# A decoder block on one core: feed-forward differences moved from GpSimd to VectorE, and one more pair of chunks in the down projection's rounds of seven products

## The chip, the core and the metric

The kernel runs on one core of one Trainium2 chip. The metric is the device time of one execution in microseconds (us): the median of three runs of the kernel before is 1283.06 us (1282.82 to 1283.29). The engines that matter are TensorE (PE in the profile; its weight loads are a row of their own, PEld), VectorE (DVE), ScalarE (ACT), GpSimd (POOL) and SyncE (SP). Each engine executes its own instructions strictly in the order in which the kernel records them, and waits at an instruction until what it needs is there.

## The reference

One layer with a feed-forward half-step at both ends; the mixing part between them is untouched by the change. For 512 tokens, model width 1024 and feed-forward width 2816:

```
def swiglu(x, w_gate, w_up, w_down):
    return (jax.nn.silu(x @ w_gate) * (x @ w_up)) @ w_down

h = h + 0.5 * swiglu(rms_norm(h, g_ffn1[i]), w_ffn1_gate[i], w_ffn1_up[i], w_ffn1_down[i])
...   # convolution module, dilated attention, gated merge
h = h + 0.5 * swiglu(rms_norm(h, g_ffn2[i]), w_ffn2_gate[i], w_ffn2_up[i], w_ffn2_down[i])
h = h + jax.nn.sigmoid(rms_norm(h, g_ple[i]) @ w_ple_gate[i]) * (p[i] @ w_ple_proj[i])
return rms_norm(h, g_final)
```

Inputs and outputs are float32.

## The kernel before

**Precision.** A float32 product is made of three matmuls on rounded halves: each operand is split into a high part (ACT copies it into a rounded type) and a low part (DVE subtracts the high part from the original). The names ending in h and l are these halves: `wh`, `wl` of a weight slab, `bh`, `bl` (or `b`, both halves in one tile) of a moving operand, `hidh`, `hidl` of a hidden chunk.

**Chunks and pairs.** The feed-forward width is 22 chunks of 128 channels, taken as 11 pairs. Gate and up are computed for a pair at a time. Pairs 0 and 1 are computed plainly (keys "gq"), while the norm is still being made. Pairs 2 to 10 are computed with seven products in place of eight (keys "gu"): the weights and the tokens are cut in two halves each way, sums and differences of the quarters are formed, and the products have the names B11, B21, T2, T1, T3, B22, T4, in this order. `quarters_of` (L712, L713, L715) records the matmuls of one product, each 128x256; a gate/up product works on four slabs of the model width and has 24 of them. Results go to three PSUM banks, pa (B11, then T2 on top, then T3, then T4), pe (B21) and pd (T1, then B22 on top). A product that accumulates on a bank may start only when the sum before has been read from it.

**The down projection** is done in `ROUNDS`, four entries (first pair, number of pairs). Round 0 is plain (`down_plain`, keys "dp"): for each of eight row blocks m, the 128x512 matmuls of all chunks of the round go to one bank (pd), and DVE adds it to the residual (L966). Rounds 1 to 3 use the seven products again (`down`, keys "dn"), in two groups of four row blocks, so 14 products a round; a product on k pairs has 6k matmuls of 128x256. After each product DVE adds the bank to the residual (`add`, L727, or L723 and L730 as two halves).

**The order** is written out by hand in `PLAN`: before, gate/up of pairs 2 to 5, round 1, pairs 6 to 8, round 2, pairs 9 and 10, the plain round, round 3. The feed-forward is executed twice with the same plan.

**Forming a pair.** A pair that goes into rounds of seven needs seven moving operands: `form_pair` makes four differences of 256 columns (`sub`, L643, two into each tile `t`) and four splits (`put`: ACT at L655, DVE at L658): B11, B21 with B22, T1 with T2, T3 with T4. Before, the differences are executed by GpSimd (`by=FORMS`, and FORMS is G). The 13 pieces of a pair are put in a list `later`; `gate_up` records some of them behind each product (`QUOTA`, 17 for a gate/up step), `down_plain` up to three behind each m, and `down` of rounds 1 and 2 takes none on its own: it only records, before a product, whatever that product still lacks. The last pair before a round is held back and formed at the start of the next gate/up step. A pair of the plain round is only split (`keep`, ACT L747 and DVE L749).

**Weights.** Slabs come by DMA from SP. For T2, T1, T3 and B22 DVE forms sums of quarters (L342, L346, L350, L355; names `s`, `wr`) and the low halves `wl` (L405), ACT the high halves (L404). For B11, B21 and T4, and for the plain round, the low half is made by ACT (L374, minus the high half) and a DMA from GpSimd's queue that adds the raw weights onto it (L376). The width of these instructions is 1024 for gate/up and for a round of four pairs, 768 for a round of three.

**Other work in the way.** In the first feed-forward the rotary tables are made by some 40 DVE instructions at L1024 (`tables`, tiles ang, n, e, nh, nl), recorded one behind several of the products and one behind each m of the plain round, from round 2 on.

## Time and profile before

| | us |
|---|---|
| median of three runs | 1283.06 |
| profiled execution, first to last instruction (span) | 1280.8 |
| TensorE busy, share of the span | 1267.4, 99% |
| VectorE busy | 1015.3, 79% |
| ScalarE busy | 740.9, 58% |
| GpSimd busy | 299.8, 23% |
| granted TensorE clock, mean | 0.998 |

The profile gives the profiled execution's own time as its span; the 2.3 us between the span and the median lie outside the first and the last instruction. The stages follow one another on TensorE: in the first feed-forward, gate/up of pair 2 starts at 52.09 us, round 1 begins near 133 us, the plain round runs from 294.52 to 317.05 us and round 3 ends near 347.9 us. In the second feed-forward the plain round runs from 1158.11 to 1180.65 us. The timeline lists each instruction by its start; matmuls are pipelined, so the distance between two starts is the pace, and the listed duration of one is its latency. DVE instructions overlap a little in the same way.

### The profile page before, as it was taken

Reading aid. Unit: us, or ns where it says so; the run is one execution under the profiler, and the core shown is the slowest. Engines: PE = TensorE matmul, PEld = TensorE weight load, DVE = VectorE, ACT = ScalarE, POOL = GpSimd, SP = SyncE. Lnnn points to the kernel's source line nnn. Section 1 sums busy time; section 2 is a strip of 40 time slices with the busy share of each in tenths; the row PEclk is TensorE's granted clock in tenths of the full one; section 3 lists DMA queues with packets and bytes.
Section 4 is the critical chain, followed back from the end, with each engine's and each line's share of the span. In section 5 each row is a group of like instructions: output and inputs, shape, how many; then the busy total and the mean of one; then the engine's idle time right before and its main releaser. Section 6 shows DMA issues by size and latency. Waiting matters only on the chain.

```text
span 1280.8 us, 21791 instructions
## 1 busy us (share of the span) xinstructions
PE 1267.4 (99%) x8266; PEld 1163.6 (91%) x8266; DVE 1015.3 (79%) x1617; ACT 740.9 (58%) x1088; POOL 299.8 (23%) x392
## 2 busy tenths in 40 slices
PE   9999999999999999999999999999999999999997
PEld 7899999998988888989898888898899999998986
DVE  6988778898969887878778755786988888786875
ACT  6677566575643264746565445373677566585662
POOL 3122222132223232333232222012122122132000
PEclk9999999999999999999999999999999999999999
DMA  9676876867879889898887788657576876867641
GB/s 302 148 171 161 204 201 157 206 165 191 193 177 227 213 152 204 155 188 150 173 183 166 168 190 218 160 119 211 132 177 159 203 206 146 208 168 187 155 115 50
DMA packets 114128, 226.12 MB, mean 177 GB/s; under 512 B 20584, under 2 KB 50664, under 8 KB 114024
## 3 DMA queue, kind: packets, MB, share of 16 engines
q0 software_dynamic: 49600, 142.10, 54.6%
q1 hardware_dynamic: 64136, 82.37, 20.1%
q8 instruction: 65, 1.06, 0.3%
q14 instruction: 39, 0.32, 0.1%
q10 hardware_dynamic: 288, 0.26, 0.1%
HBM read 168.56 MB, written 2.13 MB: 133 GB/s over the span
## 4 chain that ended last, share of the span: by engine, by line
PE 76%; DVE 2%; issue 0%; ACT 0%; DVEq 0%
PE pa L712 5%; PE pa L713 5%; PE pa L715 5%; PE pq L458 4%; PE pq L459 4%; PE pq L460 4%; PE pg L458 3%; PE pg L460 3%; PE pg L459 3%; PE pd L713 3%; PE pd L715 3%; PE pd L712 3%; PE pb L459 2%; PE pb L460 2%; PE pb L458 2%; PE pe L713 1%
## 5 line engine op out<-in xcount | busy, mean ns | idle before, releaser
L376 POOL DMA_DIRECT2D wl<-wr x108 | 93.4, 867 | 440.4 <-ACT wl L374 341.1
L712 PE MATMUL pa<-bh,wh 128*128 128x256 f32 x680 | 167.6, 284 | 0.5 <-DVE gx L727 0.4
L713 PE MATMUL pa<-bl,wh 128*128 128x256 f32 x680 | 167.3, 283 | 0.0
L1098 DVE SCALAR_TENSOR_TENSOR acc<-glu,taps,acc 128x511 f32<-128x511 f32 (+14 forms) x240 | 161.6, 732 | 0.0
L405 DVE TENSOR_TENSOR wl<-s,wh 128x1024 fp32r<-128x1024 f32 (+1 forms) x96 | 108.5, 1132 | 38.0 <-ACT wh L404 37.8
L374 ACT ACTIVATE wl<-wh 128x1024 fp32r<-128x1024 f32 x84 | 87.9, 1051 | 81.9 <-DMA wh<-in_w_in 50.8
L712 PEld LDWEIGHTS pa<-bh,wh 128*128 128x128 f32 x680 | 130.6, 192 | 1.0 <-issue 0.5
L713 PEld LDWEIGHTS pa<-bl,wh 128*128 128x128 f32 x680 | 130.8, 192 | 0.0
L374 ACT ACTIVATE wl<-wr 128x1024 fp32r<-128x1024 f32 (+1 forms) x108 | 105.7, 979 | 24.3 <-DVE wl L405 11.4
L404 ACT ACTIVATE wh<-s 128x1024 fp32r<-128x1024 f32 (+1 forms) x96 | 93.0, 969 | 38.8 <-PE pd L459 14.7
L388 ACT ACTIVATE wh<-wr 128x1024 fp32r<-128x1024 f32 (+1 forms) x108 | 105.5, 977 | 11.0 <-PE pd L715 6.1
L712 PE MATMUL pd<-bh,wh 128*128 128x256 f32 x448 | 110.3, 284 | 0.0
L713 PE MATMUL pd<-bl,wh 128*128 128x256 f32 x448 | 110.2, 283 | 0.0
L376 POOL DMA_DIRECT2D wl<-in_w_in x56 | 48.5, 869 | 219.6 <-ACT wl L374 200.5
L715 PE MATMUL pa<-bh,wl 128*128 128x256 f32 x680 | 97.0, 283 | 0.0
L458 PE MATMUL pq<-xsh,wh 128*128 128x512 f32 x224 | 88.8, 396 | 0.0
L715 PEld LDWEIGHTS pa<-bh,wl 128*128 128x128 f32 x680 | 88.4, 192 | 0.0
L459 PE MATMUL pq<-xsl,wh 128*128 128x512 f32 x224 | 87.4, 390 | 0.0
L460 PE MATMUL pq<-xsh,wl 128*128 128x512 f32 x224 | 87.4, 390 | 0.0
L713 PEld LDWEIGHTS pd<-bl,wh 128*128 128x128 f32 x448 | 86.2, 192 | 0.0
L712 PEld LDWEIGHTS pd<-bh,wh 128*128 128x128 f32 x448 | 86.1, 192 | 0.1
L458 PE MATMUL pg<-xsh,wh 128*128 128x512 f32 x192 | 76.1, 396 | 0.2 <-ACT xsh L478 0.2
(330 smaller groups left out, 3616.0 us busy)
## 6 DMA issues: line engine op xcount, KB each, us to landing
wl<-wr POOLq DMA_DIRECT2D x72, 512.0 KB, 5.7
wh<-in_w_in POOLq DMA_DIRECT2D x56, 512.0 KB, 7.0
wl<-in_w_in POOLq DMA_DIRECT2D x56, 512.0 KB, 6.0
wr<-in_w_ffn_up SPq DMA_DIRECT2D x80, 256.0 KB, 4.4
wr<-in_w_ffn_gate SPq DMA_DIRECT2D x78, 256.0 KB, 4.8
wr<-in_w_ffn_down SPq DMA_DIRECT2D x96, 192.0 KB, 3.8
wl<-wr POOLq DMA_DIRECT2D x36, 384.0 KB, 4.4
wr<-in_w_ffn_down SPq DMA_DIRECT2D x16, 256.0 KB, 4.1
```

The costliest lines, as they stand in the source:

```text
L374: A.activation(l.bitcast(F32R), h, AF.Copy, scale=-1.0)
L376: G.dma_start(to, src, accum_op=OP.add)
L388: A.activation(h, r, AF.Copy)
L404: A.activation(h, r, AF.Copy)
L405: V.tensor_sub(l, r, h.bitcast(F32))
L458: PE.matmul(ps, wh, xh, start=start, stop=False, skip_group_check=part)
L459: PE.matmul(ps, wh, xl, start=False, stop=False, skip_group_check=part)
L460: PE.matmul(ps, wl, xh, start=False, stop=stop, skip_group_check=part)
L712: PE.matmul(o, h[:, c], th, start=q in ("B11", "B21", "T1") and i == 0, stop=False, skip_group_check=True)
L713: PE.matmul(o, h[:, c], tl, start=False, stop=False, skip_group_check=True)
L715: PE.matmul(o, l[:, c], th, start=False, stop=i >= len(at) - 2, skip_group_check=True)
L1098: bg.append(lambda acc=acc, g=g, w=w, s=s: V.scalar_tensor_tensor(acc[:, s:], g[:, :S - s], w, acc[:, s:], op0=OP.mult, op1=OP.add))
```

## The change

The four differences of a pair in `form_pair` are executed by DVE instead of GpSimd. The plain round of the down projection has one pair (pair 0) instead of two; pair 1, whose gate and up are still computed plainly, is formed at the start of gate/up step 3 and goes into round 1. The rounds of seven products take pairs 1 to 3, 4 to 6 and 7 to 10, so the last has four pairs. The plan moves with them: each round comes one gate/up step earlier, and three gate/up steps lie before the plain round. The pairs held back are 4 and 7 (before 5 and 8). At the start of gate/up step 3 the waiting jobs of the plain gate/up are recorded at once, so that pair 1 is complete.

```
-ROUNDS = ((0, 2), (2, 3), (5, 3), (8, 3))
+ROUNDS = ((0, 1), (1, 3), (4, 3), (7, 4))

-PLAN = (("gu", 2), ("gu", 3), ("gu", 4), ("gu", 5), ("dn", 1, 0), ("dn", 1, 1), ("gu", 6), ("gu", 7), ("gu", 8),
-        ("dn", 2, 0), ("dn", 2, 1), ("gu", 9), ("gu", 10), ("dp", 0), ("dn", 3, 0), ("dn", 3, 1))
+PLAN = (("gu", 2), ("gu", 3), ("gu", 4), ("dn", 1, 0), ("dn", 1, 1), ("gu", 5), ("gu", 6), ("gu", 7), ("dn", 2, 0),
+        ("dn", 2, 1), ("gu", 8), ("gu", 9), ("gu", 10), ("dp", 0), ("dn", 3, 0), ("dn", 3, 1))
+PLAIN = 1
+HELD = (4, 7)
...
-    FORMS = G if FORMS_ else V
...
-    def form_pair(x1, x2, parts_, tile_=None, first_of=None, by=FORMS):
+    def form_pair(x1, x2, parts_, tile_=None, first_of=None, by=V):
...
-            if j >= EARLY:
+            if j >= PLAIN:
                 waiting.append((j, ts, tile_))
                 return
...
-                    if j not in (ROUNDS[1][0] + ROUNDS[1][1], ROUNDS[2][0] + ROUNDS[2][1]):
+                    if j not in HELD:
                         form()
...
             if key[0] == "gu":
-                if key[1] >= KF // 2 - EARLY:
-                    j = key[1] - KF // 2 + EARLY
+                while jobs and key[1] == EARLY + 1:
+                    next_job()
+                for j in range(PLAIN, EARLY) if key[1] == EARLY + 1 else range(PLAIN) if key[1] == KF // 2 - 1 else ():
                     keep(j, early[j])
                     early[j] = None
                 gate_up(key[1])
```

The order of instructions moves at three places on VectorE that the prediction speaks of. In the rows below, gx and h are the residual, L1024 of the kernel before is L1025 of the changed one.

**VectorE, round 1, first group, around the sum of product T1** (the row that reads pd). Before:

```order
L405 TENSOR_TENSOR wl_1715<-s_265_1598,wh_1714 128x768
L342 TENSOR_TENSOR s_283_1718<-wr_1632,wr_1635 128x768
L727 SCALAR_TENSOR_TENSOR gx<-pd_1627,gx 128x2x256
L346 TENSOR_TENSOR s_286_1744<-s_283_1718,wr_1638 128x768
L727 SCALAR_TENSOR_TENSOR gx<-pa_1625,gx 128x2x256
```

Now:

```order
L405 TENSOR_TENSOR wl_1476<-s_235_1357,wh_1475 128x768
L342 TENSOR_TENSOR s_253_1479<-wr_1393,wr_1396 128x768
L727 SCALAR_TENSOR_TENSOR gx<-pd_1388,gx 128x2x256
L346 TENSOR_TENSOR s_256_1505<-s_253_1479,wr_1399 128x768
L658 TENSOR_TENSOR bl_1508<-t_1355,bh_1507 128x512
L727 SCALAR_TENSOR_TENSOR gx<-pa_1386,gx 128x2x256
```

The new row at L658 is the low half of T3 and T4 of pair 3, the last pair of the round. Product T3, which follows T1 on TensorE, reads it.

**VectorE, the opening of the plain round in the first feed-forward.** Before, from the product of the two gated halves (u from p) on:

```order
L890 TENSOR_TENSOR u_3427<-p_3573,p_3536 128x2x256
L1024 SCALAR_TENSOR_TENSOR ang_2767<-n_2768,ang_2767 128x512
L876 TENSOR_TENSOR u_3427<-pa_3424,p_3459 128x2x256
L749 TENSOR_TENSOR hidl_3421<-tu_610,hidh_3420 128x512
L749 TENSOR_TENSOR hidl_3423<-tu_611,hidh_3422 128x512
L342 TENSOR_TENSOR s_566_3704<-wr_3624,wr_3627 128x768
L966 SCALAR_TENSOR_TENSOR gx<-pd_3698,gx 128x512
```

Now:

```order
L890 TENSOR_TENSOR u_3449<-p_3593,p_3557 128x2x256
L749 TENSOR_TENSOR hidl_3443<-tu_379,hidh_3442 128x512
L749 TENSOR_TENSOR hidl_3445<-tu_380,hidh_3444 128x512
L1025 SCALAR_TENSOR_TENSOR e_2536<-n_2533,e_2536 128x512
L876 TENSOR_TENSOR u_3449<-pa_3446,p_3481 128x2x256
L342 TENSOR_TENSOR s_574_3726<-wr_3642,wr_3645 128x1024
L966 SCALAR_TENSOR_TENSOR gx<-pd_3720,gx 128x512
L643 TENSOR_TENSOR t_3735<-u_3449 128x256
L643 TENSOR_TENSOR t_3735<-u_3449,t_3735 128x256
```

The low halves of the plain pair (L749) stand ahead of the row that waits for T4 (L876) instead of behind it, and the differences of pair 10 (L643) stand in VectorE's row.

**VectorE, from the last sums of the plain round to the first sum of round 3, first feed-forward.** Before:

```order
L966 SCALAR_TENSOR_TENSOR gx<-pd_3829,gx 128x512
L1024 SCALAR_TENSOR_TENSOR ang_2767<-nl_2770,ang_2767 128x512
L966 SCALAR_TENSOR_TENSOR gx<-pd_3846,gx 128x512
L1024 SCALAR_TENSOR_TENSOR ang_2767<-nh_2769,ang_2767 128x512
L405 TENSOR_TENSOR wl_3865<-s_577_3753,wh_3864 128x768
L727 SCALAR_TENSOR_TENSOR gx<-pa_3861,gx 128x2x256
```

Now:

```order
L355 TENSOR_TENSOR s_592_3811<-wr_3651,s_583_3761 128x1024
L966 SCALAR_TENSOR_TENSOR gx<-pd_3810,gx 128x512
L1025 TENSOR_SCALAR n_2533<-n_2533 128x512
L966 SCALAR_TENSOR_TENSOR gx<-pd_3821,gx 128x512
L1025 SCALAR_TENSOR_TENSOR ang_2532<-n_2533,ang_2532 128x512
L405 TENSOR_TENSOR wl_3834<-s_583_3761,wh_3833 128x1024
L727 SCALAR_TENSOR_TENSOR gx<-pa_3830,gx 128x2x256
```

The kinds of rows are the same and the slab is 1024 wide instead of 768. From u (L876) to the sum of B11 (the L727 row, on pa) there are now 31 rows on VectorE: five of 1024 columns, five of 256, two TENSOR_SCALAR at L1025, and 19 others of 512. The low half at L405 is that of product T2.

## The prediction

> **What bounds the kernel now.** I read first the page's line of engines, then the list of what TensorE waited for, then TensorE's own timeline for its pace.

> ```profile
> span 1280.8 us, 21791 instructions
> PE 1267.4 (99%) x8266; PEld 1163.6 (91%) x8266; DVE 1015.3 (79%) x1617; ACT 740.9 (58%) x1088; POOL 299.8 (23%) x392
> ...
> PE pd L459 <- DVE hidl L749: 0.6, 2, 0.4
> PE pa L712 <- DVE gx L727: 0.4, 1, 0.4
> PE pa L712 <- DVE p L884: 0.2, 1, 0.2
> ```

> TensorE is the bound nearly everywhere: in the two feed-forwards together it waited about 1.2 us (the last three rows: total, times, longest). So time can come from fewer or cheaper matmuls, and it can go wherever VectorE, off the path today, becomes late for one of them. The pace of matmuls is the distance of starts, not the listed duration:

> ```profile
> 316.38 0.39 PE L458 MATMUL pd<-hidh,wh 128*128 128x512 f32 x1
> 316.60 0.39 PE L459 MATMUL pd<-hidl,wh 128*128 128x512 f32 x1
> 316.83 0.39 PE L460 MATMUL pd<-hidh,wl 128*128 128x512 f32 x1
> 317.05 0.28 PE L712 MATMUL pa<-b,wh 128*128 128x256 f32 x1
> 317.17 0.28 PE L713 MATMUL pa<-b,wh 128*128 128x256 f32 x1
> ```

> A matmul of 512 columns takes 0.2267 us of TensorE (0.68 for three), one of 256 columns 0.12 us.

> **Term 1, the matmuls.** Per feed-forward the change takes one pair out of the plain round: two chunks, eight row blocks, three matmuls, 48 of 512 columns. It adds a pair to 14 products: six matmuls each, 84 of 256 columns. The plain round takes now (windows view; the first figure behind the window is its length):

> ```profile
> 294.52:317.05 22.53, 22.30 (x98) 17.89 (x97) 18.69 (x26) 10.03 (x14) 6.45 (x8) 1.00 0.81 191
> 1158.11:1180.65 22.54, 22.18 (x98) 17.88 (x97) 12.87 (x18) 9.92 (x14) 6.37 (x8) 1.00 0.84 203
> ```

> Its 96 matmuls need 96 x 0.2267 = 21.76, so 0.77 is lost, at its opening, where the low halves of the plain pairs stand behind the row that waits for T4. In the new order they stand ahead of it; I cost the new plain round at 48 x 0.2267 = 10.88 with nothing lost. Then 22.53 - 10.88 = 11.65 goes and 84 x 0.12 = 10.08 comes: -1.57 per feed-forward, -3.1 for both.

> [...]

> **Term 2, the differences on VectorE.** VectorE gets four differences of 256 columns for each pair of the rounds of seven, 4 x 10 pairs x 2 = 80 (72 were on GpSimd). The prices:

> ```profile
> L643 DVE TENSOR_TENSOR t<-sg,t x8: 417/419/421, 815.8 to 834.9; 128x256 f32<-128x256 f32 x8
> L643 POOL TENSOR_TENSOR t<-u x36: 731/1020/1117, 74.6 to 1168.5; 128x256 f32<-128x256 f32 x36
> ...
> L658 DVE TENSOR_TENSOR bl<-u,bh 128x512 fp32r<-128x512 f32 x18 | 30.0, 1667 | 0.0
> L658 DVE TENSOR_TENSOR bl<-t,bh 128x512 fp32r<-128x512 f32 x40 | 26.9, 685 | 1.1 <-ACT bh L655 1.1
> L658 DVE TENSOR_TENSOR b<-u,b 128x256 fp32r<-128x256 f32 x18 | 19.3, 1074 | 0.0
> L658 DVE TENSOR_TENSOR b<-t,b 128x256 fp32r<-128x256 f32 x8 | 3.4, 419 | 0.2 <-ACT b L655 0.2
> ```

> On VectorE the 80 cost 80 x 0.42 = 34 us. But the same split takes 1667 ns where GpSimd works on the same pair and 685 where it does not (1074 and 419 for the narrow one): 18 x 0.98 + 18 x 0.66 = 29.5 us of VectorE come back. VectorE's load in a gate/up step therefore hardly changes, TensorE's 20.16 us (168 x 0.12) cover it, and I cost the move at nothing there; without cover it would be the 4 x 0.33 a pair that are part of term 4. GpSimd's queue keeps only its DMAs, which are no longer behind a difference; no wait of TensorE names one of them, so that is worth nothing. The slabs of the last round are a third larger, those of the plain round half as large, the bytes in all the same.

> **Term 3, T3 of round 1 waits.** In gate/up step 3 two pairs are formed (2 and 1), 26 pieces with 17 taken; nine are left, step 4 adds the 13 of pair 3 and takes 17, so five are left when round 1 begins, among them the split of T3 and T4 of pair 3. Round 1 records them only when T3 asks. On VectorE that is behind the sum of T1, which waits for T1's last matmul, and behind one sum of weights. The rows there today, TensorE and VectorE:

> ```profile
> 141.45 0.28 PE L712 MATMUL pa<-bh,wh 128*128 128x256 f32 x1
> ...
> 142.53 0.28 PE L713 MATMUL pa<-bl,wh 128*128 128x256 f32 x1
> ...
> 142.06 0.68 DVE L727 SCALAR_TENSOR_TENSOR gx<-pd,gx 128x512 f32<-128x512 f32 x1
> 142.66 0.95 DVE L346 TENSOR_TENSOR s<-s,wr 128x768 f32<-128x768 f32 x1
> 143.82 0.69 DVE L727 SCALAR_TENSOR_TENSOR gx<-pa,gx 128x512 f32<-128x512 f32 x1 [0.21 <-PE pa L715]
> ```

> Round 1 comes a step earlier in the new plan, but the distances within it stay. T3 starts at 141.45; its tenth matmul, the first on the third pair's low half, is at 142.53. The new split comes behind the row at 142.66, so at 142.66 + 0.87 (pace of 768 columns, below) = 143.53, and is done 0.69 later, at 144.22. TensorE stands still for 144.22 - 142.53 = 1.7 us. Queued behind it are the rest of T3, B22 and T4, and nothing gives that time back, since TensorE has no idle time after. The second feed-forward has the same new order:

> ```profile
> 996.73 0.28 PE L712 MATMUL pa<-b,wh 128*128 128x256 f32 x1
> ...
> 1006.70 0.95 DVE L346 TENSOR_TENSOR s<-s,wr 128x768 f32<-128x768 f32 x1
> ```

> Round 1 starts at 996.73, T3 four products of 2.16 later at 1005.37, its tenth matmul at 1006.45; the split would end at 1006.70 + 0.87 + 0.69 = 1008.26: 1.8 us. Together +3.5. Bounds: 1.0 each if the sum of weights happens to run ahead (it can't pass in the order, but the row on pd could start 0.4 us sooner, at its product's end, and TensorE's restart is free), 2.5 each if that sum still waits for its DMA.

> **Term 4, VectorE in the short plain round.** TensorE needs 10.88 us for it instead of 22.53, while VectorE has to do the same eight sums, the sums for round 3 (now wider), the table rows, and now the differences. Paces of VectorE from successive starts, where nothing waits:

> ```profile
> 265.23 1.23 DVE L405 TENSOR_TENSOR wl<-s,wh 128x1024 fp32r<-128x1024 f32 x1
> 266.37 1.22 DVE L342 TENSOR_TENSOR s<-wr,wr 128x1024 f32<-128x1024 f32 x1
> ...
> 301.54 0.42 DVE L658 TENSOR_TENSOR b<-u,b 128x256 fp32r<-128x256 f32 x1
> 301.87 0.42 DVE L1024 TENSOR_SCALAR n<-n 128x512 f32<-128x512 f32 x1
> ...
> 309.11 0.68 DVE L1024 SCALAR_TENSOR_TENSOR e<-n,e 128x512 f32<-128x512 f32 x1
> 309.71 0.94 DVE L350 TENSOR_TENSOR wr<-wr,wr 128x768 f32<-128x768 f32 x1
> 310.58 0.68 DVE L966 SCALAR_TENSOR_TENSOR gx<-pd,gx 128x512 f32<-128x512 f32 x1
> ```

> So 1.14 us for 1024 columns, 0.87 for 768, 0.60 for 512, 0.33 for 256 and for a TENSOR_SCALAR. From u (on pa) to the sum of B11 the new row of VectorE has 31 instructions: 5 x 1.14 + 19 x 0.60 + 7 x 0.33 = 19.4 us. Ahead of them:

> ```profile
> 293.23 0.69 DVE L890 TENSOR_TENSOR u<-p,p 128x512 f32<-128x512 f32 x1 [0.70 <-ACT p L889]
> ```

> Three rows of 512 columns follow it now (two low halves, one table row), so u on pa starts at 293.23 + 4 x 0.60 = 295.63 and the sum of B11 is read at 295.63 + 19.4 = 315.0. Product T2 accumulates on the same bank and needs that row, and the low half one row earlier. TensorE would come to T2 at 294.52 + 10.88 + two products of 2.88 = 311.16. It waits 3.9 us. I take +3.9 for the first feed-forward; bounds 2.5 (if the opening loses nothing to the three rows) and 6 (if rows of this stretch wait for ACT or a DMA). In the second there are no table rows: eight fewer in the stretch (six of 512 columns, two at 0.33: 4.3 us) and one ahead of it, so VectorE begins u 0.5 us behind the opening and B11's sum is read at 0.5 + 15.1 = 15.6; T2 comes at 10.88 + 5.76 = 16.64: no wait, with 1.0 to spare.

> One more thing can be late in that stretch: the low half for B21, which ACT makes behind the split of T3 and T4 of pair 10 in its own order, after which a DMA adds to it (issue to landing: median for this size, then least, median and most over all of L376).

> ```profile
> wl<-wr POOLq DMA_DIRECT2D x72, 512.0 KB, 5.7
> ...
> DMA to landing us min/median/max: 3.9/5.5/11.2
> ```

> The last difference comes at 0.5 + 6.9 (12 rows up to it: 2 x 1.14 + 5 x 0.60 + 5 x 0.33) = 7.4 in the second feed-forward, two ACT instructions (some 0.6 and 1.0) and the 5.7 to landing put the half at about 15, and B21 needs it at 10.88 + 2.88 + 16 x 0.12 = 15.7. I take +0.2 for it, bounds 0 and 2; in the first it is later by some 1.5, but ends ahead of T2's wait.

> **Sum.** -3.1 + 3.5 + 3.9 + 0.2 = +4.5 on the span of 1280.8, so 1285.3; the 2.3 us between span and median stay, **1287.5 us**, 0.35% slower. Less than 0.2% (2.6 us) can't be told from no change here.

> **Rivals.**
> 1. Only term 3 waits: VectorE's row in the plain round is shorter than I count, because nothing disturbs it any more and it enters the round early. For it: 29.5 us come back, and VectorE was idle before some rows of the plain round. Against it: the 31 rows have nothing to wait for in my count already, and they sum to 8.5 us more than the round lasts. It decides if VectorE reaches u 4 us sooner, which T4 forbids. 1283.06 - 3.1 + 3.5 = 1283.5, the same as before.
> 2. Neither waits, the other side: the split of T3 and T4 is done before TensorE comes to it, and the round as well, so only term 1 remains: 1283.06 - 3.1 = 1279.9, faster by 0.25%. The point from which it decides is 142.53 of the old trace: the split must be through VectorE by then, but its row stands behind the sum of T1, which reads what ends at 141.45. Only if TensorE's order asked for pair 3 much later would this hold.
> 3. The waits are worse: in both feed-forwards the low half of B21 lands late, since ACT is held in order by differences that come late, and the DMA takes longer than its median. For it: the longest of these DMAs took 11.2. Against it: a wait of T2 in the first feed-forward already covers some 3 us of such a delay. Two or three us more in each plain round give 1287.3 + 4 to 6, 1291 to 1293.
> 4. The change doesn't do what it says to VectorE: the long splits (1667 ns) have another reason than GpSimd, and 29.5 us don't come back. For it: GpSimd still issues DMAs from the same engine. Against it: the splits of differences (685) ran while it issued some. Then a pair costs VectorE 1.6 us more (0.98 + 0.66); a gate/up step still hides that, the first plain round does not: 1287.5 + 1.6 = 1289.1.

> **How the numbers follow.** The forecast with both waits 0.62, rival 1 0.13, rival 2 0.07, rivals 3 and 4 together 0.18. The range reaches down to rival 1 and up into rival 3: 1283 to 1291.5; outside it are rival 2 and the end of rival 3. Faster 0.07 (rival 2), the same 0.18 (rival 1 and the low end of the forecast, below 1285.6), slower 0.75.

> **What would show it.** Right: round 1 with a gap of 1.5 to 2 us inside T3 in each feed-forward, released by DVE at L658; a gap of about 4 us ahead of T2 of round 3 in the first only, released by L727 or L405; the plain round near 10.9 with no gap at its opening; no split above 0.75 us. Wrong: T3 without a gap (the split came in time after all), a wait at T2 in both feed-forwards (the DMA or ACT, not the table rows), or a wait in a gate/up step, which I cost at nothing.

## The result and the profile after

The changed kernel takes 1293.36 us (median of five runs, 1289.92 to 1294.43), the kernel before in the same comparison 1283.06 us: a ratio of 1.0075, 95% interval 1.0063 to 1.0087. It is slower, as forecast, but by 10.3 us where 4.4 were forecast, and outside the range of 1283.0 to 1291.5. The profiled execution took 1291.49 us. (In the comparison that the first four experiments below share, one run with the late pieces flushed took 1373.24 us at a mean clock of 0.849 and one of the kernel before 2343.28 us at 0.831; both are left out of the ratios.) Its line of engines, and what TensorE waited for (total, times, longest):

```profile
span 1289.7 us, 21920 instructions
PE 1269.4 (98%) x8338; PEld 1168.2 (91%) x8338; DVE 1016.1 (79%) x1701; ACT 743.5 (58%) x1092; POOL 244.5 (19%) x320
...
PE pa L712 <- ACT bh L655: 2.5, 2, 1.2
PE pa L712 <- DVE gx L727: 2.0, 1, 2.0
PE pd L460 <- DMA wl<-wr: 1.3, 1, 1.3
PE pe L715 <- DMA wl<-wr: 1.3, 1, 1.3
...
PE pa L713 <- DVE bl L658: 0.7, 2, 0.3
PE pa L712 <- ACT p L871: 0.7, 2, 0.5
```

Of these rows only gx stood in the list of before, with 0.4. VectorE's busy time is the same as before (1016.1 against 1015.3). TensorE's timeline shows where the new stops are; a stop is given below by the distance of starts less the pace, so a little more than the bracket says:

```profile
122.64 0.28 PE L713 MATMUL pa<-bl,wh 128*128 128x256 f32 x1
124.15 0.38 PE L712 MATMUL pa<-bh,wh 128*128 128x256 f32 x1 [1.23 <-ACT bh L655]
124.88 0.38 PE L713 MATMUL pa<-bl,wh 128*128 128x256 f32 x1 [0.34 <-DVE bl L658]
...
126.73 0.41 PE L712 MATMUL pd<-bh,wh 128*128 128x256 f32 x1
126.94 0.41 PE L713 MATMUL pd<-bl,wh 128*128 128x256 f32 x1
...
264.30 0.38 PE L712 MATMUL pa<-bh,wh 128*128 128x256 f32 x1 [0.50 <-ACT p L871]
301.70 0.50 PE L460 MATMUL pd<-hidh,wl 128*128 128x512 f32 x1 [1.28 <-DMA wl<-wr]
320.98 0.35 PE L712 MATMUL pa<-bh,wh 128*128 128x256 f32 x1 [2.02 <-DVE gx L727]
1184.90 0.38 PE L715 MATMUL pe<-bh,wl 128*128 128x256 f32 x1 [1.26 <-DMA wl<-wr]
```

The first three rows are T3 of round 1 in the first feed-forward: it stops for 1.39 and 0.61 us. The second feed-forward has the same pair of stops at 995.21 and 995.93 (1.39 and 0.60). Then come a gate/up step (0.66; two more of 0.32 and 0.33 at 276.23 and 285.30), the third matmul of the plain round (1.44), T2 of round 3 in the first feed-forward (2.28), and B21 of round 3 in the second (1.42).

The rows at 126.73 and 126.94 show something else: matmuls of 256 columns are 0.21 us apart, not 0.12. The view by windows has the granted TensorE clock behind the five engines' busy times (then DMA share and GB/s):

```profile
118.37:121.78 3.41, 3.41 (x30) 3.41 (x30) 2.95 (x5) 0.92 (x2) 0.00 (x0) 1.00 1.03 260
121.78:125.19 3.41, 1.83 (x13) 1.44 (x12) 2.93 (x4) 2.83 (x4) 0.91 (x2) 1.00 0.29 63
125.19:128.60 3.41, 3.41 (x18) 3.41 (x17) 1.56 (x2) 0.84 (x1) 0.78 (x1) 0.50 1.04 189
128.60:132.01 3.41, 3.41 (x31) 3.41 (x30) 1.56 (x2) 0.85 (x1) 0.00 (x0) 1.00 0.29 79
...
992.18:995.59 3.41, 2.18 (x16) 1.78 (x15) 3.36 (x6) 2.54 (x4) 0.85 (x1) 1.00 0.16 59
995.59:999.01 3.42, 3.08 (x25) 3.08 (x26) 1.91 (x4) 1.40 (x3) 0.84 (x1) 1.00 1.03 188
```

Behind the stop of the first feed-forward the clock is 0.50 for 3.41 us. With starts 0.213 us apart some 16 matmuls begin in it, where 28 would at 0.12: 1.5 us lost. (The counts in the rows include matmuls that only reach into a window. The expectations below take 1.7 for such a window, half of its length; the starts give 1.5.) Behind the same stop in the second feed-forward the clock stays at 1.00. In the profiled execution of the kernel before it is 1.00 from its first record, at 5 us, to the last 6 us.

The plain rounds in the same view, the first feed-forward and the second:

```profile
299.79:312.83 13.04, 11.75 (x50) 8.83 (x49) 12.80 (x22) 8.22 (x12) 3.38 (x4) 1.00 0.75 170
1167.75:1178.64 10.89, 10.89 (x50) 9.06 (x49) 10.86 (x18) 8.45 (x12) 3.38 (x4) 1.00 0.82 183
```

And the differences and splits on VectorE (groups with their mean in ns):

```profile
L643 DVE TENSOR_TENSOR t<-u,t 128x256 f32<-128x256 f32 x36 | 15.1, 421 | 0.5
L643 DVE TENSOR_TENSOR t<-u 128x256 f32<-128x256 f32 x36 | 15.1, 418 | 0.0
L658 DVE TENSOR_TENSOR bl<-u,bh 128x512 fp32r<-128x512 f32 x18 | 12.3, 684 | 0.0
L658 DVE TENSOR_TENSOR b<-u,b 128x256 fp32r<-128x256 f32 x18 | 7.5, 418 | 0.0
```

### The profile page after: what moved, and what is told of

Read it like the earlier page. It is cut to its first block, busy times and chain, and to the rows that moved or that the text cites. A ratio compares the mean times of both kernels' runs of the same rounds, so it can differ in the third digit from the quotient of the medians.

```text
span 1289.7 us, 21920 instructions
## 1 busy us (share of the span) xinstructions
PE 1269.4 (98%) x8338; PEld 1168.2 (91%) x8338; DVE 1016.1 (79%) x1701; ACT 743.5 (58%) x1092; POOL 244.5 (19%) x320
## 3 DMA queue, kind: packets, MB, share of 16 engines
q8 instruction: 66, 1.08, 0.4%
## 4 chain that ended last, share of the span: by engine, by line
PE 71%; DVE 3%; issue 2%; DMA 2%; ACT 1%; DVEq 0%; POOL 0%; POOLq 0%; ACTq 0%; SPq 0%
PE pa L712 5%; PE pa L715 5%; PE pa L713 5%; PE pq L458 4%; PE pq L459 4%; PE pq L460 4%; PE pg L458 3%; PE pg L459 3%; PE pg L460 3%; PE pd L715 2%; PE pd L713 2%; PE pd L712 2%; PE pb L460 2%; PE pb L458 2%; PE pb L459 2%
## 5 line engine op out<-in xcount | busy, mean ns | idle before, releaser
L376 POOL DMA_DIRECT2D wl<-wr x108 | 92.6, 859 | 564.1 <-ACT wl L374 313.5
L712 PE MATMUL pa<-bh,wh 128*128 128x256 f32 x704 | 174.0, 284 | 5.4 <-ACT bh L655 2.5
L713 PE MATMUL pa<-bl,wh 128*128 128x256 f32 x704 | 173.4, 283 | 0.7 <-DVE bl L658 0.7
L405 DVE TENSOR_TENSOR wl<-s,wh 128x1024 fp32r<-128x1024 f32 (+1 forms) x96 | 110.7, 1153 | 48.6 <-ACT wh L404 48.4
L712 PEld LDWEIGHTS pa<-bh,wh 128*128 128x128 f32 x704 | 135.0, 192 | 7.0 <-ACT bh L655 2.9
L713 PEld LDWEIGHTS pa<-bl,wh 128*128 128x128 f32 x704 | 135.1, 192 | 1.1 <-DVE bl L658 1.1
L374 ACT ACTIVATE wl<-wh 128x1024 fp32r<-128x1024 f32 x84 | 88.0, 1050 | 61.9 <-DMA wh<-in_w_in 39.9
L374 ACT ACTIVATE wl<-wr 128x1024 fp32r<-128x1024 f32 (+2 forms) x108 | 104.7, 969 | 22.1 <-DVE wl L405 6.0
L712 PE MATMUL pd<-bh,wh 128*128 128x256 f32 x464 | 114.9, 284 | 0.0
L713 PE MATMUL pd<-bl,wh 128*128 128x256 f32 x464 | 114.7, 284 | 0.0
L388 ACT ACTIVATE wh<-wr 128x1024 fp32r<-128x1024 f32 (+2 forms) x108 | 104.5, 967 | 14.0 <-DMA wl<-wr 7.0
L715 PE MATMUL pa<-bh,wl 128*128 128x256 f32 x704 | 100.4, 284 | 0.0
L715 PEld LDWEIGHTS pa<-bh,wl 128*128 128x128 f32 x704 | 91.8, 193 | 0.0
L712 PEld LDWEIGHTS pd<-bh,wh 128*128 128x128 f32 x464 | 89.8, 193 | 0.0
L713 PEld LDWEIGHTS pd<-bl,wh 128*128 128x128 f32 x464 | 89.7, 193 | 0.0
L376 POOL DMA_DIRECT2D wl<-in_w_in x56 | 47.7, 851 | 221.3 <-ACT wl L374 211.2
L458 PE MATMUL pq<-xsh,wh 128*128 128x512 f32 x224 | 88.7, 396 | 0.0
L459 PE MATMUL pq<-xsl,wh 128*128 128x512 f32 x224 | 87.3, 390 | 0.0
L460 PE MATMUL pq<-xsh,wl 128*128 128x512 f32 x224 | 87.3, 390 | 0.0
L458 PE MATMUL pg<-xsh,wh 128*128 128x512 f32 x192 | 76.2, 397 | 0.2 <-ACT xsh L478 0.2
## 6 DMA issues: line engine op xcount, KB each, us to landing
wl<-wr POOLq DMA_DIRECT2D x76, 512.0 KB, 5.5
wh<-in_w_in POOLq DMA_DIRECT2D x56, 512.0 KB, 7.5
wl<-in_w_in POOLq DMA_DIRECT2D x56, 512.0 KB, 6.1
```

The source lines that it names most:

```text
L374: A.activation(l.bitcast(F32R), h, AF.Copy, scale=-1.0)
L376: G.dma_start(to, src, accum_op=OP.add)
L388: A.activation(h, r, AF.Copy)
L405: V.tensor_sub(l, r, h.bitcast(F32))
L458: PE.matmul(ps, wh, xh, start=start, stop=False, skip_group_check=part)
L459: PE.matmul(ps, wh, xl, start=False, stop=False, skip_group_check=part)
```

## The experiments

The theory after the result: the waits come from the new order (pieces recorded too late, too much VectorE work in a plain round of half the length, low halves whose lead is counted in slabs that now last half as long), and a stop of about 2 us sometimes halves TensorE's clock for a while (of those of 2.00, 1.99 and 2.28 us above, the first). The rivals: the engine of the differences makes the stops, or the waits only move when one is removed, or the clock has nothing to do with the stops.

**The late pieces of pair 3.**

```
...
             last = r == len(ROUNDS) - 1
+            if r == 1 and g_ == 0:
+                flush(later)
...
```

> The changed kernel, with the five pieces of pair 3 that are still unrecorded taken ahead of the first product of round 1 instead of on demand inside T3. Waits only: the two stops of T3 (1.39 + 0.61 us in the first feed-forward, 1.39 + 0.60 in the second) go, 4.0 us: 1293.4 - 4.0 = 1289.4. Waits and clock (a stop of about 2 us is followed, in some six cases of ten, by some 3.4 us at half the TensorE clock, 1.7 us): 2 x 0.6 x 1.7 = 2.0 more, 1287.4, and no window near 125 us with a granted clock of 0.5. If pair 3's pieces only move the wait elsewhere (to T2, behind the sum of B11): 1292 to 1293.

Measured: 1289.54 us, ratio 1.0049 (1.0035 to 1.0063). Both stops of T3 are gone, and with them the half clock at 125 us. What TensorE waits for now:

```profile
PE pa L712 <- DVE gx L727: 3.2, 2, 2.4
PE pa L712 <- DVE h L730: 2.0, 2, 1.1
```

Of the h row one wait, 1.1, is old; it lies between the feed-forwards, in the kernel before too. The five pieces now stand ahead of the sum of B11, and T2 of round 1 stops for 0.96 and 1.02 us, half of what was gained. T2 of round 3 stopped for 2.69 here, and this time it was that stop which a window of half clock followed (319.40 to 322.82). So the order is the cause, and flushing all five at once moves half of the wait. That the median meets the forecast of waits alone (1289.4) is luck: by the stops of the two profiles only some 2 us of the 3.8 are gained. The mean clocks of the runs (0.996 to 0.998, against 0.995 to 0.998 without the edit) suggest that fewer windows of half clock make the rest; that is inferred.

**The table rows in the plain round.**

```
-TABLES_P = 1
-TABLES_D = {"B21": 1, "T3": 1, "B22": 1, "T4": 1}
+TABLES_P = 0
+TABLES_D = {q: 1 for q in PRODUCTS}
```

> The changed kernel, with no table row recorded in the plain round; they go behind all products of rounds 2 and 3 instead of four of seven. If the wait of T2 in the first feed-forward (2.28 us) comes from VectorE's long row: it goes, 1293.4 - 2.3 = 1291.1, with the clock theory 1.1 less, 1290.0; the stop at the plain round's third matmul (1.44) stays. If it comes from the DMA of a low half, nothing changes: 1293.4.

Measured: 1288.28 us, 1.0041 (1.0027 to 1.0054). No wait of T2 is left in round 3 of the first feed-forward, so VectorE's row was its cause. B21's low half, which T2's stop had covered, now shows (1.08):

```profile
PE pa L712 <- ACT bh L655: 2.5, 2, 1.2
PE pe L715 <- DMA wl<-wr: 2.1, 2, 1.2
PE pd L460 <- DMA wl<-wr: 1.7, 2, 1.5
```

The gain, 5.1 us between the medians, is larger than the waits that went, and larger than either forecast. The best spans of the two kernels, with a clock of 0.998 and 0.999, are 1288.2 and 1286.0: 2.2 us. The rest would be the number of half-clock windows that a run meets, which is inferred from the mean clocks.

**Both edits**, and **both with longer leads**: `LEAD` of B21 from 3 to 5, `NEXT` from 3 to 5.

> Both edits together. Waits only: 1293.4 - 4.0 - 2.3 = 1287.1. Waits and clock: 1293.4 - 4.0 - 2.3 - 3.1 = 1284.0, a granted clock of 0.998 as before, runs within 0.5 us of each other. Left are 1.44 + 1.42 at low halves by DMA and about 1.0 in gate/up step 8.

> Both edits, and the low halves made by ACT and a DMA started up to five slabs ahead (B21, and the plain round's slabs during gate/up) instead of three. If the two stops of 1.4 us at such halves are a matter of the lead in slabs, that slabs of half the time shorten: both go, 1284.0 - 2.9 = 1281.1, faster than before. If ACT is the one that is late, or the early halves take its time in gate/up, the stops stay or move: 1284 to 1286.

Measured: 1285.80 us (1.0019, 1.0010 to 1.0028) and 1284.66 us (1.0011, 1.0003 to 1.0020). The first is neither of its forecasts: that with the clock, 1284.0, did not count the 2.0 us that move to T2 of round 1 (0.96 and 1.02 here too), and with them it would be 1286.0. With no stop above 1.3 us left, the runs of the first agree within 1.6 us (five of the changed kernel spread over 4.5) and no window but the last has less than full clock. The longer leads remove the stops at the plain round's halves (1.09, 0.35 and 0.48) and at B21 of the second feed-forward (0.64), so these were a matter of the lead. At B21 of the first a stop of 1.57 came in their place: its half was issued about as late as without the longer lead (307.37 against 308.00) and took 7.4 us to land, and TensorE now came sooner. A wait of 0.54 us is new, between the two feed-forwards at 844.80; the versions with `NEXT` 5 have it and those with 3 don't. The gain of 1.1 is less than the 2.9 expected.

**The engine of the differences alone**, once in the changed kernel (`by=G` in `form_pair`) and once in the kernel before (`FORMS_ = False`, so VectorE):

> The changed kernel with its differences back on GpSimd; rounds and order as changed. If the engine of the differences is worth nothing, as predicted (34 us of VectorE against 29.5 regained from splits), the same stops stay: 1292 to 1294, splits of u at 1667 and 1074 ns again. If VectorE's extra rows made the stops: the waits at p in gate/up steps 8 to 10 (0.66 + 0.32 + 0.33) and part of T2's wait go, 1290 to 1291. If GpSimd's differences hold up its DMAs: above 1295.

> The kernel before with its differences on VectorE and nothing else changed. Predicted: worth nothing in gate/up, 1283.1; splits of u near 685 and 419 ns instead of 1667 and 1074. If VectorE is too full in the gate/up steps that also carry table rows: 0.3 to 1.3 us of waits at p there, 1283.5 to 1284.5. If the long splits have another reason than GpSimd: they stay at 1667 and VectorE's busy time rises by 34 us.

Measured: 1294.54 us (1.0089, 1.0075 to 1.0103) for the changed kernel with GpSimd, and 1282.25 us (0.9993, 0.9984 to 1.0002) for the kernel before with VectorE. In the first, these rows:

```profile
PE pe L715 <- DMA wl<-wr: 5.3, 2, 3.2
...
PE pa L713 <- DVE bl L658: 1.7, 2, 0.9
...
L658 DVE TENSOR_TENSOR bl<-u,bh 128x512 fp32r<-128x512 f32 x18 | 29.1, 1618 | 0.0
L658 DVE TENSOR_TENSOR b<-u,b 128x256 fp32r<-128x256 f32 x18 | 14.5, 807 | 0.0
```

and in the second:

```profile
L658 DVE TENSOR_TENSOR bl<-u,bh 128x512 fp32r<-128x512 f32 x18 | 12.3, 684 | 0.0
```

The long splits follow GpSimd's differences in both kernels. The stops of T3 are there with either engine (1.7 and 1.8 us with GpSimd). With GpSimd the low halves for B21 come later still: stops of 3.37 and 2.20 us. T2 does not wait, but it stands behind the stop of 3.37, in which VectorE goes on. Why that half is late shows on GpSimd and ScalarE:

```profile
307.13 1.02 POOL L643 TENSOR_TENSOR t<-u,t 128x256 f32<-128x256 f32 x1
...
308.18 0.63 ACT L655 ACTIVATE bh<-t 128x512 fp32r<-128x512 f32 x1 [1.00 <-POOL t L643]
308.71 1.04 ACT L374 ACTIVATE wl<-wr 128x1024 fp32r<-128x1024 f32 x1
...
310.06 0.86 POOL L376 DMA_DIRECT2D wl<-wr  x1 [1.91 <-ACT wl L374]
```

ScalarE makes the half (L374) behind a split that waits for GpSimd's last difference. So its DMA is issued 12.57 us behind the opening of the plain round, against 11.72 in the changed kernel; in the second feed-forward it is 11.04 against 9.57. The loss of the change thus belongs to its plan: in the new plan the two engines differ by less than their runs spread (1294.54 and 1293.36), and in the kernel before the move to VectorE is worth 0.9 us if anything.

**The waits taken out one by one.** One more piece of pair 3 behind each product of gate/up step 4; table rows from round 1 on, behind the products of the rounds only; `NEXT` 5, `LEAD` of B21 4:

```
...
-                for _ in range(min(QUOTA.get(q, 0), len(later))):
+                for _ in range(min(QUOTA.get(q, 0) + (j == EARLY + 2), len(later))):
...
-TABLES = {"B21": 1, "T3": 1, "B22": 1, "T1": 1}
+TABLES = {}
...
-                if n == "1" and key[1:] == (2, 0):
+                if n == "1" and key[1:] == (1, 0):
...
```

> The changed kernel with one more piece of pair 3 taken behind each product of gate/up step 4, so that none is left for round 1; table rows only in the rounds of seven (from round 1 on, one behind each product), none in gate/up or the plain round; low halves of the plain round up to five slabs ahead in gate/up, of B21 four. Waits of the run with both edits that should go: T2 of round 1, 0.96 + 1.02; p in steps 8 to 10, 1.04; plain halves 1.09 + 0.35 + 0.48; B21 0.64. 1285.8 - 5.6 = 1280.2, which is the 3.1 of the matmuls and no new stop. If the table rows in rounds 1 and 2 make VectorE late for a sum there: 1282 to 1284.

Measured: 1281.78 us, ratio 0.9988 (0.9979 to 0.9997), against 1283.15 for the kernel before. All the stops named are gone, those in the gate/up steps too. What TensorE waits for in the seven products now:

```profile
PE pa L712 <- DVE gx L727: 1.1, 3, 0.7
PE pa L712 <- DVE h L730: 0.7, 2, 0.4
```

VectorE is late for some sums of the rounds (0.38, 0.84, 0.31, 0.27 and 0.44 by the starts), and the wait of 0.55 between the feed-forwards has come with `NEXT`. Of the 3.1 us that the matmuls save 1.4 remain. A second version of the spreading (extra pieces behind the first four products of steps 3 and 4, no table row behind B11 and T2) was to remove those as well:

> As the spread version, but the extra pieces are taken behind the first four products of gate/up steps 3 and 4, and no table row stands behind B11 and T2. If the remaining waits at sums of round 1 and 2 (0.38 + 0.84 + 0.31 + 0.27, and 0.44 in the second feed-forward) come from table rows and late pieces: 1281.8 - 2 = 1280. If they come from VectorE's own load in a round: 1281.5 to 1282.

Measured: 1281.92 us, 0.9991 (0.9982 to 1.0000). Of the waits at sums above 0.25 us one of 0.31 is left, but one of 0.56 and one of 0.57 came in gate/up step 3 of the two feed-forwards, behind VectorE's row at p (L884). What the earlier pieces delay there was not looked into; the first version stands.

**The clock.** 30 deliberate stops, one ahead of B21 in each gate/up step and each group of the down projection. The first try let a chain of small GpSimd operations hold a small matmul:

```
...
+        G.tensor_sub(dm, src[:, :64], one[:, :64])
+        for i in range(n):
+            G.tensor_sub(dm, dm, one[:, :64])
+        PE.matmul(to[:, :64], one, dm, start=True, stop=True)
...
```

> The run with both edits, and 30 deliberate stops of TensorE: ahead of B21 in every gate/up step and every group of the down projection, one small matmul waits for a chain of 3, 9, 6, 15 or 12 small GpSimd operations in turn, some 1 to 4 us. It adds work, no result depends on it. If the clock is set for the next 3.4 us by how busy TensorE was in the last 3.4 us, in windows that run on without regard to the stops: stops under 1.7 us are never followed by half clock, longer ones when 1.7 us or more of them lie in one window, those of 3 us nearly always, and each half-clock stretch lasts 3.4 us and begins on one grid of 3.41 us. If a stop's length alone decides: one length divides those followed from those not. If it has nothing to do with stops: half-clock stretches also elsewhere.

The stops came out at 5 to 10 us, where some 1 to 4 were meant, so no length was short enough to tell the theories apart (1582.5 us, and half clock behind every stop). But the half-clock stretches were 3.41 us, or two, three or four times that, and all began at whole multiples of 3.41 us from each other; this is called the grid below. The second try used a chain on ScalarE (`A.activation(dm, dm, AF.Copy)`, 3 to 13 of them) in the spread version:

> The spread version, with 30 deliberate short stops of TensorE: ahead of B21 in every gate/up step and every group of the down projection one small matmul waits for a chain of 3 to 13 small ScalarE operations, some 1 to 3 us. It adds work, no result depends on it. Grid theory (from the long stops): half-clock stretches are whole windows of 3.41 us on one grid; a window is granted half clock where TensorE stood for about half of the window before it or more. Then stops below some 1.7 us are never followed by one; of those of 2 us about six in ten are, of 2.5 us seven, of 3 us nearly nine; which ones follows from where the grid cuts them. Rival, length alone: one length divides them, wherever they lie.

The stops were up to 6.0 us long, most of them between 1.5 and 5. The windows of the grid around two of them, in the columns as above:

```profile
1194.63:1198.04 3.41, 2.48 (x21) 2.27 (x19) 2.67 (x5) 0.11 (x1) 0.00 (x0) 1.00 0.88 204
1198.04:1201.45 3.41, 1.80 (x15) 1.80 (x16) 0.96 (x1) 3.25 (x9) 0.09 (x1) 1.00 0.78 247
1201.45:1204.87 3.42, 3.42 (x30) 3.42 (x30) 2.01 (x5) 1.93 (x3) 0.76 (x1) 1.00 0.63 132
...
225.24:228.66 3.42, 1.52 (x13) 1.31 (x11) 1.69 (x3) 3.29 (x9) 0.00 (x0) 1.00 0.94 238
228.66:232.07 3.41, 1.06 (x5) 1.06 (x6) 0.77 (x3) 3.16 (x10) 0.00 (x0) 0.50 0.39 140
```

The stop that ended at 1199.65 lasted 2.70 us, but the grid cuts it into 1.09 and 1.61, and the clock stays at 1.00. A stop of 2.35 us that ended at 255.09 lay wholly in one window, and half clock followed. Length alone does not decide. The last two rows show the first part of another stop, of 4.41 us: 2.06 us of it lie in the window from 225.24, and the next has half clock. Sorted by the time without a matmul (by starts, delays under 0.1 us left out), the 11 full-clock windows with 0.9 to 1.9 us are all followed by full clock, the 26 with 2.06 us or more all by half clock. Behind windows that had half clock themselves less was enough: in the two runs with deliberate stops those with up to 0.81 us are followed by full clock, those with 0.87 or more by a further half-clock window. All half-clock stretches of this run begin at whole multiples of 3.4133 us from the first at 57.99, to within 0.01 us over 1386 us. The two of the changed kernel, from 125.19 and, behind the last matmul, from 1285.72, lie 1160.53 us apart, 340 times 3.4133.

The other runs agree. In the changed kernel the window from 121.78 held 2.00 us of stop (followed by half clock), the one from 992.18 only 1.65, the rest falling into the next (not followed); T2's 2.28 were cut into 1.04 and 1.24. With GpSimd's differences a window held 1.92 and was not followed, with the table rows out one held 1.99 and was. A delay of some 0.1 us at a restart (0.22 between the starts at 995.93 and 996.15 in the changed kernel, where the pace is 0.12) can be counted in or left out, so the boundary is known no better than that: near 2 us of 3.41. The expectations took half a window, 1.7 us, for the boundary and so six cases in ten for a stop of 2 us, which no run showed; with 2 us it would be some four in ten, (3.41 - 2.0) / 3.41, an estimate from the windows above. (The busy column overstates these windows: each matmul ahead of a stop counts with its latency of 0.28 to 0.38, not its pace of 0.12.)

## Why the prediction was right in sign and wrong in size

The step that failed is the sum: it took every wait at its bare length and set other losses at nothing, or nearly so. The span of the profiled execution, 1289.7, lies 4.4 us above the forecast of 1285.3. Of these, 1.5 are a window of half clock, for which there was no term; 1.2 are B21's low half in the second feed-forward, taken at 0.2 and measured at 1.42; about 1.0 are waits in gate/up steps, which the text cost at nothing and itself named as a sign of being wrong; 0.5 are T3. Small differences elsewhere make up the rest. The median lies another 1.9 us above the profiled execution. The mean clocks point to more windows of half clock in those runs, but they have no trace, so that part stays open.

- **Bound and pace of matmuls (term 1): right.** The plain round of the second feed-forward is 10.89 us, with no gap at its opening, against 10.88 in the text. The spread version, where most of the stops are gone, is faster than before, as the term says (its stages are given below).
- **Differences (term 2): right in the prices, wrong that nothing comes of it in gate/up.** 0.42 us each, the splits at 684 and 418 ns, VectorE's total unchanged. But three stops at p came in gate/up steps of the first feed-forward, 1.31 us against 0.34 at one place before: about +1.0. They are gone in the spread version, which among other things takes the table rows out of those steps; with GpSimd's differences 0.22 and 0.33 are left, and the kernel before with VectorE's has none. So the new plan and the differences both have a part in them, and the table rows probably; this was not taken apart further. That the move takes work off GpSimd's path is worth nothing in the old plan only: in the new one GpSimd's differences cost 5.6 us at B21, through the split on ScalarE, where 1.42 are lost without them.
- **T3 of round 1 (term 3): right in place and mechanism, too small.** 4.0 us instead of 3.5. The restart, free by the text's bounds, took some 0.1 more (0.22 from 995.93 to 996.15, against 0.12). The text made VectorE's row late and looked at the low half alone; ScalarE's high half, which the matmul before needs, is late first. Its copy of T3 and T4 stands behind the two halves of the next slab in its order, and the first of these began only when T1 freed its buffer:

```profile
122.00 0.85 ACT L374 ACTIVATE wl<-wr 128x768 fp32r<-128x768 f32 x1 [1.31 <-PE pd L715]
122.75 0.83 ACT L388 ACTIVATE wh<-wr 128x768 fp32r<-128x768 f32 x1
123.49 0.61 ACT L655 ACTIVATE bh<-t 128x512 fp32r<-128x512 f32 x1
...
124.13 0.69 DVE L658 TENSOR_TENSOR bl<-t,bh 128x512 fp32r<-128x512 f32 x1
```

- **VectorE in the short plain round (term 4): right.** u on pa began 1.12 us behind the opening (1.11 in the text) and the sum of B11 19.24 us after it (19.4). TensorE's stops up to T2 sum to 3.9 us, as forecast, though in three pieces: 1.44 and 0.17 at low halves of the plain round, which the text had not seen, and 2.28 at T2, which would otherwise have been longer by as much. Delays of 0.1 to 0.2 us add 0.5 (4.4 in the table below). The second feed-forward had no wait of T2.
- **B21's low half in the second feed-forward: 1.42, taken as 0.2.** It lies inside the bounds of 0 to 2; the value was wrong. The sum had the half in time by 0.7 us, with the median of 5.7 from issue to landing. The issue came 9.57 us behind the opening, about as forecast (7.4 + 0.6 + 1.0), but this DMA landed 7.5 us later, at 1184.86:

```profile
1177.32 0.85 POOL L376 DMA_DIRECT2D wl<-wr  x1 [1.70 <-ACT wl L374]
```

- **What had no term: the clock.** 1.5 us in the profiled execution, and by their clocks more in others. The five spans of the changed kernel, 1288.2, 1289.7, 1291.6, 1292.6 and 1292.7, go with mean clocks of 0.998, 0.997, 0.996, 0.995 and 0.995, and the window of half clock from 125.19, full of 256-column matmuls, cost 1.5. Only the second of these executions has a trace (one window), so that the slower ones met two or more is inferred from their clocks.

By stages, from one first matmul to the next, the profiled execution against that of before (us):

| stage | forecast | measured | made of |
|---|---|---|---|
| to gate/up 2 | 0 | +0.41 | waits at the start, which differ by execution |
| gate/up and rounds 1, 2 | +1.7 | +4.86 | T3 2.0, clock 1.5, gate/up 1.0, shorter delays 0.4 |
| plain round and round 3 | +2.3 | +2.80 | -1.57, and 4.4 lost where 3.9 was forecast |
| up to gate/up 2 of the second | 0 | -0.59 | delays below 0.25 us each, not looked into |
| gate/up and rounds 1, 2 | +1.8 | +2.16 | T3 2.0 |
| plain round and round 3 | -1.4 | -0.02 | -1.57, B21 1.42 |
| the rest | 0 | -0.75 | a wait of 0.75 us at 1212.21 is gone |
| sum | +4.5 | +8.9 | |

In the spread version the plain round and round 3 together are 1.37 and 1.45 us shorter than before, which is the -1.57 of term 1 but for small waits.

- **Rivals.** Rival 1 is out: the first plain round and round 3 lost the time of term 4. Rival 3 came nearest to the size (1291 to 1293), but its cause, the late halves, made only 1.2 of the 4.4 us by which the profiled execution exceeds the forecast. Rival 4 is out, the long splits go with GpSimd's differences (684 ns without them, 1618 with them in the same plan). Rival 2, no wait at all, is nearest to what the spread version makes of the change (1281.8 against its 1279.9, with sums in the rounds still late).

## What to carry to other kernels

Where TensorE never waits, price a new wait at its length and, from about 2 us on, at a further 1.5 us (measured in the window from 125.19) times the chance that so much of it falls into one stretch of the grid. Two short stops in one stretch counted together here: T3's 1.39 and 0.61 lay in one, and half clock followed. T2's single stop of 2.28 was cut into 1.04 and 1.24, and half clock did not follow. When a stage is cut to half its length, recount everything whose lead is counted in steps of that stage (early slabs, rows recorded behind each step), since the leads shrink with it. A list that is emptied on demand shows up as a stall inside the product that asks; spread its rest over the step before, a little behind each product, rather than all at once.
